# State space output of a hybrid layer: products packed by channel pair, one activation per batch instead of sixteen

## The chip, the core and the metric

One core of a Trainium2 chip runs the whole program. The metric is the device time of one execution in microseconds, the median of three runs. The engines are named as the profile names them: PE is TensorE (matrix products; PEld are its weight loads), DVE is VectorE, ACT is ScalarE, POOL is GpSimd, SP is SyncE, which here only issues transfers.

## The reference, cut to what matters

One decoder layer with two parallel groups, a state space group (SSM) and a latent attention group (MLA), then a gated MLP. The change touches the last step of the SSM group:

```
s_re, s_im = associative_scan(...)            # 64 channel groups of 16, state of 64 each
y = (einsum('lbgp,ghp->blgh', s_re, c_re)
     - einsum('lbgp,ghp->blgh', s_im, c_im)
     + d_skip * u)
y = gelu(y)                                   # 256 tokens x 1024 channels
y_ssm = y * sigmoid(y @ w_glu + b_glu)
```

## The kernel before, in words

The layer has 256 tokens and 2048 channels, in float32 throughout. A large product is made of three: each 128x1024 chunk of weights is split by ACT (`hi`, line 150) and DVE (`lo`, line 151), and PE multiplies in the order of lines 165, 166 and 168. Before about 284 us the program is the input projection, the attention with the SSM beside it, and the output projections; after it come the up and down products of the MLP (lines 175, 177 and 1132), where PE hardly waits.

The SSM's 64 groups are 32 pairs, worked through in 8 batches b of 4 pairs q. A pair has 32 channels. The scan runs over 64 blocks i of 4 tokens j. Of each batch the functions do this:

- `ssm_v` (line 533): PE, 16 products into a bank `psv`, out of `gm`, which DVE transposes in `ssm_in_mats` (line 490).
- `ssm_k` (line 544): PE, 8 products of 32 columns; `ssm_m` (lines 557, 561) makes out of them the matrix `mt`, by DVE and 8 copies of ACT.
- `ssm_rot` (lines 571 to 587): rotation and scan on DVE, ending in `sh` (line 587); `ssm_back` (lines 595 to 599): POOL turns it back into the states `spv`.
- `ssm_y` (lines 610 to 619): the output. It adds three products, `mt` by the inputs `u4`, and the matrix `clp` by both halves of `spv`, into a bank `psy`, and ACT writes gelu of it into `yT`.

`ssm_main` strings these together in three steps per batch; `pace()` takes steps between the chunks of the other work, by a table of digits (`STEPS`). The order in which each engine finally gets its instructions is set by the framework's scheduler when the program is built, by its own estimate of when each could run; on the chip each engine runs its list strictly in that order. So a change of one function moves instructions of others.

Around the SSM stand: the last steps of the attention heads (lines 921 to 955; `macc` collects the sums of squares on POOL); `tok_sums`, `tok_rsqrt`, `tok_rows` (lines 260, 267, 268, 275), which turn `macc` into the scale row `rr` (copied by ACT at line 998); `out_mla` (lines 165 to 168 on tiles `ym`, then DVE at lines 1000 and 1001), whose results wait in three `mm` banks for `rr`; and, when all of `yT` is there, its split into `yhl` (lines 1018, 1019) and eight products with `w_glu` (lines 165 to 168 on tiles `yhl`), whose squares POOL adds into `sacc`, summed by PE at line 260.

Of the kernel before, what the change touches and what calls it, by code (L numbers as in the profile page):

```python
# [14 lines left out]
AF = mybir.ActivationFunctionType  # L15
# [8 lines left out]
T = 256  # L24
# [30 lines left out]
def layer_kernel(ctx: ExitStack, tc: tile.TileContext, pack, pos, xt, bk, w_in, w_kpe, w_uqn,  # L55
                 w_uqp, w_kn, w_v, w_glu, w_out, w_up, w_down, final_w, out):
    nc = tc.nc
    V, A, G_, PE, SP = nc.vector, nc.scalar, nc.gpsimd, nc.tensor, nc.sync
# [10 lines left out]
    def wk_bank():  # L69
        return psw.tile([P, 512], F32, tag="wk", name="wk")  # L70
# [440 lines left out]
    u4_ = [None]  # L511
# [12 lines left out]
    psvs, psks, yT = {}, {}, [None]  # L524
# [76 lines left out]
    def ssm_y(b):  # L601
        if b == 0:
            yT[0] = mid.tile([P, 8, T], F32, tag="mB", name="yT")
        qs = slice(4 * b, 4 * b + 4)
        m, s, clp = mt[b % 2], spv[b % 2], clps[b % 4]
        psy = wk_bank().rearrange("p (q i) -> p q i", i=64)
        for q in range(4):
            for hf in range(2):
                hp = slice(64 * hf, 64 * hf + 64)
                PE.matmul(psy[hp, q], m[:, q, 2 * hf:2 * hf + 2].rearrange("p j n -> p (j n)"),  # L610
                          u4_[0][:, b, q, :], start=True, stop=False)
                for c in range(2):
                    PE.matmul(psy[hp, q],
                              clp[:, c, q, 2 * hf:2 * hf + 2].rearrange("p l g h -> p (l g h)"),
                              s[:, c, q, :], start=False, stop=(c == 1))
        for q in range(4):
            dst = yT[0][32 * q:32 * q + 32, b].rearrange("p (i j) -> p j i", j=4)
            for j in range(4):
                A.activation(dst[:, j], psy[32 * j:32 * j + 32, q], AF.Gelu_apprx_tanh)  # L619

    def ssm_main():

        for b in range(9):
            ssm_load(b + 1)
            if b < 8:
                ssm_v(b)
            if b < 7:
                ssm_out_mats(b + 1, 0)
            yield
            if b < 8:  # L630
                ssm_rot(b)
                ssm_k(b)
            if b < 7:
                ssm_in_products(b + 1)
                ssm_out_mats(b + 1, 1)
            yield
            if b > 0:
                ssm_y(b - 1)
            if b < 8:
                ssm_back(b)  # L640
                ssm_m(b)
            if b < 7:
                ssm_in_mats(b + 1)
            yield
# [109 lines left out]
    for i, (ct, hf) in enumerate(u_order):  # L754
# [12 lines left out]
        if i >= 7:  # L767
            while done:
                c = done.pop(0)
# [132 lines left out]
    def scratch(kind):  # L902
        o, n = ring[kind]
        turn[kind] ^= 1
        o += n * turn[kind]
        return scr[:, o:o + n]
# [137 lines left out]
    for ct in range(16):  # L1044
# [3 lines left out]
        t = scratch("t")  # L1048
# [17 lines left out]
    for i in range(44):  # L1066
        pgv = [mm_bank(), wk_bank()]
        a = abuf[i % 2]
        for gv, hf in up_order(i):
# [3 lines left out]
            if hf == 1:  # L1073
                t = fp.tile([P, T], F32, tag=f"cv{gv}", name="low")
# [7 lines left out]
        for gv in range(2):  # L1082
            ch_ = 44 * gv + i
            t = fp.tile([P, T], F32, tag=f"cv{gv}", name="cv")
# [198 lines left out]
```

## Time and profile before

| | |
|---|---|
| time, median of 3 runs | 1097.57 us (1096.87 to 1098.04) |
| the profiled execution: its time, its span | 1098.27 us, 1096.4 us |
| busy over the span: PE, PEld | 1053.3 us (96%), 930.4 us (85%) |
| DVE, ACT, POOL | 771.4 us (70%), 626.7 us (57%), 269.6 us (25%) |

How to read it: the shares are means over the span. PE is close to always busy, but its 4% of idle time is not spread evenly, and neither is the work of the others; what the change can move lies in the first quarter of the span, so the rows below are cut by stage. A row of a timeline gives the start, how long the merged instructions took from the first start to the last end, the engine, the line, what it writes and reads, how many were merged (x16), and in brackets how long the engine had sat idle before it, and for whom. A float32 product shows as two records of PE, each with a weight load of its own. PEclk is the share of TensorE's full clock of 2.4 GHz that was granted; the lower level is 1.2 GHz, so 0.92 is a mixture.

### The profile page before, as it was taken

Reading aid. Unit: us, or ns where it says so; the run is one execution under the profiler, and the core shown is the slowest. Engines: PE = TensorE matmul, PEld = TensorE weight load, DVE = VectorE, ACT = ScalarE, POOL = GpSimd, SP = SyncE. Lnnn points to the kernel's source line nnn. Section 1 sums busy time; section 2 is a strip of 40 time slices with the busy share of each in tenths; the row PEclk is TensorE's granted clock in tenths of the full one; section 3 lists DMA queues with packets and bytes.
Section 4 is the critical chain, followed back from the end, with each engine's and each line's share of the span. In section 5 each row is a group of like instructions: output and inputs, shape, how many; then the busy total and the mean of one; then the engine's idle time right before and its main releaser. Section 6 shows DMA issues by size and latency. Waiting matters only on the chain.

```text
span 1096.4 us, 18029 instructions
## 1 busy us (share of the span) xinstructions
PE 1053.3 (96%) x6856; PEld 930.4 (85%) x6856; DVE 771.4 (70%) x1085; ACT 626.7 (57%) x1074; POOL 269.6 (25%) x284
## 2 busy tenths in 40 slices
PE   7979999878999999999999999999999999999997
PEld 7978878777999888888888888888888888888896
DVE  8999898697799677676767676676768445454543
ACT  6567688947766565555655555555555434343433
POOL 8371645674234111111121212111111000000000
PEclk9989999999999999999999999999999999999999
DMA  6645432542655566666666666666666976666662
GB/s 211 220 116 182 141 115 78 173 134 79 198 179 185 171 195 192 189 192 184 191 183 195 190 190 186 184 193 188 193 182 187 247 247 187 188 184 191 213 190 77
DMA packets 56663, 195.24 MB, mean 178 GB/s; under 512 B 6528, under 2 KB 8448, under 8 KB 56576
## 3 DMA queue, kind: packets, MB, share of 16 engines
q1 hardware_dynamic: 54576, 190.93, 56.8%
q10 hardware_dynamic: 2000, 3.16, 1.3%
q8 instruction: 54, 0.88, 0.3%
q14 instruction: 33, 0.27, 0.1%
HBM read 189.86 MB, written 2.10 MB: 175 GB/s over the span
## 4 chain that ended last, share of the span: by engine, by line
PE 78%; DVE 10%; ACT 6%; issue 3%; DMA 3%; POOL 0%; ACTq 0%; SPq 0%; DVEq 0%
PE mm L175 15%; PE wk L175 15%; PE mm L1132 11%; PE wk L1132 11%; PE wk L177 8%; PE mm L177 8%; PE mm L168 3%; PE mm L166 3%; PE mm L165 3%; DVE lo L151 2%; ACT yT L619 2%; DMA raw<-in_w_in_dram 1%; ACT hi L150 1%; DVE epad L486 1%; PE wk L922 1%
## 5 line engine op out<-in xcount | busy, mean ns | idle before, releaser
L151 DVE TENSOR_TENSOR lo<-raw,hi 128x1024 fp32r<-128x1024 f32 x329 | 411.0, 1251 | 267.5 <-ACT hi L150 259.9
L150 ACT CAST hi<-raw 128x1024 fp32r<-128x1024 f32 x329 | 343.8, 1048 | 320.4 <-PE wk L1132 113.3
L1093 POOL TENSOR_TENSOR cv<-cv 128x256 f32<-128x256 f32 x44 | 51.6, 1173 | 395.5 <-ACT cv L1092 395.5
L175 PE MATMUL mm<-x2b,hi 128*128 128x512 f32 x352 | 88.3, 392 | 0.0
L175 PE MATMUL wk<-x2b,hi 128*128 128x512 f32 x352 | 88.3, 392 | 0.0
L175 PE MATMUL mm<-x,hi 128*128 128x512 f32 x352 | 88.2, 392 | 0.0
L175 PE MATMUL wk<-x,hi 128*128 128x512 f32 x352 | 88.1, 392 | 0.0
L1132 PE MATMUL wk<-hi,hid 128*128 128x512 f32 (+1 forms) x360 | 88.0, 364 | 0.0
L1132 PE MATMUL mm<-hi,hid 128*128 128x512 f32 x312 | 85.5, 396 | 0.0
L1132 PEld LDWEIGHTS wk<-hi,hid 128*128 128x128 f32 x360 | 63.5, 188 | 13.0
L175 PEld LDWEIGHTS wk<-x2b,hi 128*128 128x128 f32 x352 | 63.4, 189 | 11.3
L175 PEld LDWEIGHTS mm<-x,hi 128*128 128x128 f32 x352 | 63.3, 189 | 11.3
L175 PEld LDWEIGHTS mm<-x2b,hi 128*128 128x128 f32 x352 | 63.3, 189 | 11.3
L175 PEld LDWEIGHTS wk<-x,hi 128*128 128x128 f32 x352 | 63.3, 189 | 11.3
L1132 PEld LDWEIGHTS mm<-hi,hid 128*128 128x128 f32 x312 | 57.8, 188 | 13.2 <-ACT hi L150 0.2
L177 PEld LDWEIGHTS mm<-x2b,lo 128*128 128x128 f32 x352 | 48.1, 190 | 3.4
L177 PEld LDWEIGHTS wk<-x,lo 128*128 128x128 f32 x352 | 48.0, 190 | 3.4
L177 PEld LDWEIGHTS mm<-x,lo 128*128 128x128 f32 x352 | 48.0, 190 | 3.4
L177 PEld LDWEIGHTS wk<-x2b,lo 128*128 128x128 f32 x352 | 48.0, 190 | 3.4
L1132 PE MATMUL wk<-lo,hid 128*128 128x512 f32 (+1 forms) x180 | 50.9, 364 | 0.0
L165 PE MATMUL mm<-xh,hi 128*128 128x256 f32 x184 | 47.9, 294 | 2.5 <-ACT hi L150 2.5
L1094 ACT CAST hid<-cv 128x256 fp32r<-128x256 f32 x44 | 17.9, 406 | 55.6 <-POOL cv L1093 55.6
(345 smaller groups left out, 2152.6 us busy)
## 6 DMA issues: line engine op xcount, KB each, us to landing
raw<-in_w_up_dram SPq DMA_DIRECT2D x176, 512.0 KB, 3.7
raw<-in_w_down_dram SPq DMA_DIRECT2D x88, 512.0 KB, 3.7
raw<-in_w_out_dram SPq DMA_DIRECT2D x32, 512.0 KB, 3.7
raw<-in_w_in_dram SPq DMA_DIRECT2D x25, 512.0 KB, 4.0
bkt<-in_bk_dram SPq DMA_DIRECT2D x8, 512.0 KB, 5.6
raw<-in_w_glu_dram SPq DMA_DIRECT2D x8, 512.0 KB, 4.2
raw<-in_w_uqn_dram SPq DMA_DIRECT2D x4, 512.0 KB, 4.0
hT<-in_xt_dram SPq DMA_DIRECT2D x4, 512.0 KB, 5.3
```

What stands on the lines that cost most here:

```text
L150: A.copy(hi, raw)
L151: V.tensor_tensor(out=lo, in0=raw, in1=hi.bitcast(F32), op=ALU.subtract)
L165: PE.matmul(ps, wh(k), xh(k), start=(first and k == 0), stop=False)
L166: PE.matmul(ps, wh(k), xl(k), start=False, stop=False)
L168: PE.matmul(ps, wl(k), xh(k), start=False, stop=(last and k == nk - 1))
L175: PE.matmul(ps, wh(k), xp(k), start=(first and k == 0), stop=False)
L177: PE.matmul(ps[:, n:], wl(k), xp(k)[:, 0], start=False, stop=(last and k == nk - 1))
L486: V.tensor_tensor(out=epad[:, :, g, :, g, :], in0=ev1[:, :, g], in1=ev2[:, :, g], op=ALU.add)
L619: A.activation(dst[:, j], psy[32 * j:32 * j + 32, q], AF.Gelu_apprx_tanh)
L1093: G_.tensor_tensor(out=cv[0], in0=cv[0], in1=cv[1], op=ALU.mult)
L1094: A.copy(hid[0][:, i, :], cv[0])
L1132: PE.matmul(ps[:, 0:n], hid[x][:, 2 * i + k, ts_], w[wk][:, 512 * k + c0:512 * k + c0 + n], start=(i == 0 and s == 0 and k == 0), stop=(i ...
```

## The change

Before, the two tokens of a half (hf) were taken together: a product gave 64 partitions (2 tokens of 32 channels) of `psy`, at a place in the bank for each pair q. Each piece of 32 partitions by 64 columns then had to go to other partitions of `yT`, so ACT needed 16 activations of 32x64. Now each product gives one token j of one pair q, 32 partitions by 64 columns, at partitions 32q, where `yT` has that pair; 48 products take the place of 24, and one activation of 128x256 that of 16. Summed values and their order stay.

```diff
-        psy = wk_bank().rearrange("p (q i) -> p q i", i=64)
-        for q in range(4):
-            for hf in range(2):
-                hp = slice(64 * hf, 64 * hf + 64)
-                PE.matmul(psy[hp, q], m[:, q, 2 * hf:2 * hf + 2].rearrange("p j n -> p (j n)"),
-                          u4_[0][:, b, q, :], start=True, stop=False)
-                for c in range(2):
-                    PE.matmul(psy[hp, q],
-                              clp[:, c, q, 2 * hf:2 * hf + 2].rearrange("p l g h -> p (l g h)"),
-                              s[:, c, q, :], start=False, stop=(c == 1))
-        for q in range(4):
-            dst = yT[0][32 * q:32 * q + 32, b].rearrange("p (i j) -> p j i", j=4)
-            for j in range(4):
-                A.activation(dst[:, j], psy[32 * j:32 * j + 32, q], AF.Gelu_apprx_tanh)
+        psy = wk_bank()[:, 0:T].rearrange("p (j i) -> p j i", j=4)
+
+        for j in range(4):
+            for t in range(3):
+                for q in range(4):
+                    w = m[:, q, j] if t == 0 else clp[:, t - 1, q, j].rearrange("p g h -> p (g h)")
+                    PE.matmul(psy[32 * q:32 * q + 32, j], w, u4_[0][:, b, q, :] if t == 0 else s[:, t - 1, q, :],
+                              start=(t == 0), stop=(t == 2))
+        A.activation(yT[0][:, b].rearrange("p (i j) -> p j i", j=4), psy, AF.Gelu_apprx_tanh)
```

The file is five lines shorter below this place: a line L1000 of before is L995 after, and the output's lines 610, 613 and 619 become 612, 612 and 614. The scheduler, given other lengths for these instructions, orders the engines' lists anew between about 130 and 310 us. Two places matter.

The first is DVE's list from the reciprocal of `tok_rsqrt` (line 268) on, where `out_mla`'s first results are taken out of their banks (lines 1000 and 1001; 995 and 996 after). Before:

```order
L268 RECIPROCAL rtok<-rtok 128x2
L151 TENSOR_TENSOR lo<-raw,hi 128x1024 x3
L1000 TENSOR_TENSOR scr<-mm,rr 128x256 x2
L578 TENSOR_TENSOR ta<-wk,tabc 128x512
L579 TENSOR_TENSOR tb<-wk,tabc 128x512
L480 TENSOR_TENSOR e_2474<-bkt,wkk 128x512
L557 TENSOR_TENSOR wk<-wk,bkt 32x2x32
L1001 TENSOR_TENSOR hT<-hT,scr 128x256 x2
```

and now:

```order
L268 RECIPROCAL rtok<-rtok 128x2
L151 TENSOR_TENSOR lo<-raw,hi 128x1024 x2
L995 TENSOR_TENSOR scr<-mm,rr 128x256 x2
L996 TENSOR_TENSOR hT<-hT,scr 128x256 x2
L578 TENSOR_TENSOR ta<-wk,tabc 128x512
L579 TENSOR_TENSOR tb<-wk,tabc 128x512
L480 TENSOR_TENSOR e_2501<-bkt,wkk 128x512
L557 TENSOR_TENSOR wk<-wk,bkt 32x2x32
```

One of three `lo` has moved behind the first results. From line 268 to the last scan (line 587 of batch 7) DVE's list held 11 each of `lo`, `scr` and `hT`, and now holds 10 of each; the eleventh stand behind the scan.

The second is the end of ACT's list in this stage: the copies to the last `mt` (line 561, batch 7), the gelu of batches 6 and 7, and the split of `yT` (line 1018; 1013 after). Before:

```order
L561 COPY mt_125<-wk 32x2x128 x2
L561 COPY mt_125<-wk 32x2x96
L619 ACTIVATE yT<-wk 32x64 x16
L561 COPY mt_125<-wk 32x2x96
L561 COPY mt_125<-wk 32x2x64 x2
L561 COPY mt_125<-wk 32x2x32 x2
L150 CAST hi<-raw 128x1024
L1018 CAST yhl<-yT 128x512 x3
L150 CAST hi<-raw 128x1024 x2
L619 ACTIVATE yT<-wk 32x64 x16
L1018 CAST yhl<-yT 128x512
```

and now:

```order
L561 COPY mt_125<-wk 32x2x128 x2
L561 COPY mt_125<-wk 32x2x96 x2
L561 COPY mt_125<-wk 32x2x64 x2
L561 COPY mt_125<-wk 32x2x32 x2
L614 ACTIVATE yT<-wk 128x4x64
L150 CAST hi<-raw 128x1024
L1013 CAST yhl<-yT 128x512 x3
L150 CAST hi<-raw 128x1024
L614 ACTIVATE yT<-wk 128x4x64
L1013 CAST yhl<-yT 128x512
```

The copies now stand together ahead of batch 6's gelu, and one `hi` fewer stands ahead of batch 7's. In PE's list, counted the same way, 240 of the 128x256 products of lines 165 to 168 stand between `rr`'s products (line 275) and the end of batch 7's output products, where there were 260. From there on to the sum of `sacc` (line 260), which was the 259th product on, there are now 275, and the sum itself stands 7 products further ahead in the work: 282 to the same place.

## Rows read from the trace of the kernel before

**Rows 1.** By stage: length, busy PE, PEld, DVE, ACT, POOL, clock, DMA share, GB/s

```profile
130.00:184.00 54.00, 51.30 (x387) 42.09 (x387) 49.62 (x100) 40.94 (x100) 30.82 (x34) 1.00 0.38 118
...
184.00:205.40 21.40, 17.74 (x224) 16.33 (x222) 9.22 (x22) 20.24 (x61) 10.50 (x14) 0.92 0.34 124
205.40:262.00 56.60, 47.04 (x613) 43.93 (x613) 56.09 (x77) 34.66 (x93) 41.46 (x40) 0.94 0.40 122
...
262.00:284.00 22.00, 18.77 (x161) 17.27 (x160) 11.61 (x17) 18.87 (x49) 4.00 (x4) 0.92 0.36 125
```

**Rows 2.** Timeline of ACT around the scale row rr

```profile
198.26 4.64 ACT L619 ACTIVATE yT<-wk 32x64 f32<-32x64 f32 x16
202.92 1.28 ACT L267 ACT_TABLE_LOAD   x1
...
207.21 0.37 ACT L998 COPY rr<-wk 128x256 f32<-128x256 f32 x1
```

**Rows 3.** Timeline of DVE: behind rtok, and the last scan

```profile
204.51 0.17 DVE L268 RECIPROCAL rtok<-rtok 128x2 f32<-128x2 f32 x1 [7.14 <-ACT rtok L267]
205.44 4.83 DVE L151 TENSOR_TENSOR lo<-raw,hi 128x1024 fp32r<-128x1024 f32 x3 [0.77 <-ACT hi L150]
210.19 0.74 DVE L1000 TENSOR_TENSOR scr<-mm,rr 128x256 f32<-128x256 f32 x2
...
260.56 1.22 DVE L587 TENSOR_TENSOR_SCAN sh<-d,vh 128x512 f32<-128x512 f32 x1
```

**Rows 4.** Groups by line and shape: count, busy us, mean ns, idle before

```profile
L151 DVE TENSOR_TENSOR lo<-raw,hi 128x1024 fp32r<-128x1024 f32 x102 | 133.2, 1310 | 41.3 <-ACT hi L150 34.7 <-PE mm L168 2.9 <-ACT r L282 1.9
...
L619 ACT ACTIVATE yT<-wk 32x64 f32<-32x64 f32 x128 | 35.6, 278 | 8.3 <-PE wk L613 6.8
...
L1001 DVE TENSOR_TENSOR hT<-hT,scr 128x256 f32<-128x256 f32 x16 | 10.7, 678 | 0.0
...
L1000 DVE TENSOR_TENSOR scr<-mm,rr 128x256 f32<-128x256 f32 x16 | 6.4, 414 | 0.1
...
L953 ACT ACTIVATE scr<-wk 128x256 f32<-128x256 f32 x8 | 3.2, 395 | 3.5 <-PE wk L951 3.4
```

**Rows 5.** Timeline of ACT, POOL and PE in the last two batches

```profile
261.70 4.61 ACT L619 ACTIVATE yT<-wk 32x64 f32<-32x64 f32 x16
...
265.35 0.73 POOL L599 TENSOR_TENSOR spv<-td,tc__3122 128x252 f32<-128x252 f32 x1
...
277.47 0.62 PE L165 MATMUL mm<-yhl,hi 128*128 128x256 f32 x3 [1.77 <-ACT yhl L1018]
...
305.63 0.50 PE L260 MATMUL wk<-ones,sacc 128*128 128x1 f32 x4
```

**Rows 6.** Timeline of PE: small products, and full ones, without a wait

```profile
189.58 0.60 PE L950 MATMUL wk<-scr,qv 128*128 128x256 f32 x2
190.02 0.38 PE L951 MATMUL wk<-scr,qv 128*128 128x128 f32 x2
...
204.82 0.68 PE L275 MATMUL wk<-ident,rtok 128*128 128x128 f32 x4 [0.65 <-DVE rtok L268]
205.44 1.15 PE L533 MATMUL wk<-u,gm 128*64 128x64 f32 x32
206.52 1.07 PE L544 MATMUL wk<-clp,bkt 128*32 128x128 f32 x16
207.51 0.33 PE L610 MATMUL wk<-u,mt 128*64 128x64 f32 x2
...
208.85 0.45 PE L613 MATMUL wk<-spv,clp 128*64 128x64 f32 x6
...
288.47 1.12 PE L168 MATMUL mm<-yhl,lo 128*128 128x256 f32 x8
```

**Rows 7.** Timeline of PE behind batch 0's output; waits of PE, 184 to 282 us

```profile
139.59 0.38 PE L165 MATMUL mm<-chl,hi 128*128 128x256 f32 x1 [1.66 <-ACT qpt L889]
...
PE wk L533 <- DVE gm L490: 7.4, 3, 3.1
```

## The prediction

> **What bounds the kernel now.** I read the stages first [rows 1], then the timelines of the engine that each stage names. The change touches only about 130 to 284 us; behind it PE works without a pause, so whatever PE starts earlier there ends earlier at the end.
>
> - 130 to 184 us: PE is busy 51.30 of 54.00 us, ACT only 40.94. PE is the bound.
> - 184 to 205.4 us: ACT is busy 20.24 of 21.40 us and is the bound; two of the eight gelu blocks lie here. One of them stands right in the way [rows 2]: the activations of batch 2 from 198.26 to 202.92, and only then the root `rtok`. DVE waits 7.14 us for it [rows 3].
> - 205.4 to 262 us: DVE is busy 56.09 of 56.60 us. It is the bound; ACT has 22 us to spare. PE waits, 7.4 us in three waits for `gm`, which comes from DVE [rows 7].
> - 262 to 284 us: DVE drops to 11.61 of 22.00, ACT is busy 18.87. Batch 6's 16 activations [rows 5], from 261.70 to 266.31, cut the copies to the last `mt` in two, batch 7's follow, and PE waits 1.77 us for the last split at 277.47.
>
> **Part by part.**
>
> *Gelu.* 128 activations at 278 ns, 35.6 us in all; back to back, 16 take 4.64 us [rows 2, 4]. The nearest single activation of 128x256 out of a bank is line 953 at 395 ns [rows 4]. The strided write into `yT` may cost more: all of the 278 ns by its 64 columns, taken four times, would be 1.1 us. I take 0.45, since the 395 reads as many values from the same memory; ACT is freed of about 4.2 us a batch. In the first stage this hides behind PE, in the third behind DVE; it counts in the second and fourth.
>
> *The products.* Each batch had 48 records on PE and now has 96, each still streaming 64 columns. Before, they took from 207.51 to 209.30, 1.79 us [rows 6]. What do records of 32 partitions cost? No row has them with four column groups taking turns. The neighbours [rows 6]: line 533, 64 columns, two groups in turn: (1.15 - 0.22)/31 = 30 ns per record, the 0.22 being one record's own length. Line 544, 128 columns, two groups of 32: (1.07 - 0.27)/15 = 53 ns. A full-width product, 256 columns: line 951 starts 0.44 us after line 950's two records, 220 ns each, so 55 ns for 64 columns if nothing runs beside it. Hence the ends: no overlap, 96 x 55 ns and some 0.35 us to start and drain = 5.6 us; four side by side, 96 x 14 ns and 0.35 = 1.7 us. I take 30 ns, the rate of line 533, as the closest in columns streamed and in width: 96 x 0.030 + 0.35 = 3.2 us, **1.4 us more per batch** (ends -0.1 and 3.9).
>
> Lines 533 and 544 show 64 columns at 30 ns and 128 at 53, so the columns streamed set the pace there. The Trainium skill ("TensorEngine Tiling (Array Packing)", Performance Considerations) says that a product has about 60 cycles of overhead, so that one of a single column takes as long as one of 60, and that the tiling factor should not be taken from a dimension that is already small; this speaks against the change. By its 60 cycles at 2.4 GHz, 25 ns by estimate, a batch would take 2.75 us and cost 1.0 more. No run here shows the floor yet.
>
> *130 to 184 us.* Batch 0's products become 1.4 us longer, ahead of a wait of 1.66 us of PE for ACT [rows 7], which hides them; without that cover they would cost all 1.4. Gain and loss: 0.
>
> *184 to 205.4 us.* ACT gives up 8.4 of 20.24 us. The next bound is PE: 17.74 busy and 2 x 1.4 make 20.5 of 21.40 [rows 1], so the products of line 275 come only about 1 us earlier, ending at 204.4 in place of 205.5 [rows 6], and `rr`, 0.37 us [rows 2], at 204.8. But what stood between is gone: before, three `lo` (4.83 us) came between the root and the first `scr`, at 210.19 [rows 3], because their `hi` wait on ACT behind the root. With `rtok` no longer behind 16 activations, the two `lo` that still stand ahead run while PE works, and `scr` starts at 204.8.
>
> *205.4 to 262 us.* From that `scr` to the last scan's end, 261.78, DVE had 51.6 us without a pause [rows 3]. The third `lo` now lies in it, +1.3; and one `lo`, `scr` and `hT` each of the list have gone behind the scan, -(1.3 + 0.4 + 0.7) = -2.4 by their means [rows 4]. So the scan ends at 204.8 + 51.6 + 1.3 - 2.4 = 255.3, if DVE need never wait for PE. PE has 47.04 [rows 1] + 4 x 1.4 - 20 moved products at 0.12 us (eight records of line 168 start within 0.84 us of each other [rows 6]) = 50.2 us of work in 50.9: next to no slack, although a clock of 0.94 in that stage [rows 1] may give back up to 3 us of it if PE idles less. I charge 2 us of DVE waiting for PE: 257.3, a gain of 4.5.
>
> *262 us on.* After the scan POOL needs 4.3 us for the last `spv` (266.08 against 261.78 [rows 3, 5]), then the products 3.2 us: 264.8. Gelu and the last split follow while PE works off what remains of the chunks, so its waits here go. To the place of the sum of `sacc` PE has 282 products at 0.12 us, 33.8 us: 298.6 instead of 305.63 [rows 5].
>
> The sum: **7 us less**. Made against the profiled execution, 1098.27 us (its span is 1096.4), which is 0.7 above the median of 1097.57, that is 1091.3; against the median, **1090.5**.
>
> **The rivals.**
>
> 1. *Four groups truly side by side.* Then the products cost what they did. For it: line 544, 32 wide, paces itself by half the full-width rate with two groups, so four may halve it again. Against: 30 ns is the smallest spacing in these rows. PE no longer bounds 184 to 205.4 (1.4 x 2 = 2.8 us come back), the 2 us charged for DVE's waits go, and batch 7's own 1.4: 7 + 6 = 13 us, 1084.5. The Trainium skill (same page, Performance Considerations, on column tiling) gives up to 4x for products of 32 columns. That is this rival.
>
> 2. *The products don't overlap, the other side.* At 55 ns per record a batch costs 3.9 us more; PE's work in the second and third stage becomes 17.74 + 7.8 and 47.04 + 15.6 - 2.4, 85.8 us in 78: 8 us more, and batch 0's pokes 2.2 out of its cover; against that stands up to 5 us of waits in the tail. About 5 us slower, 1102.5. It decides from where the added time eats PE's waits: 3.66, 9.56 and 3.2 us idle in the last three stages [rows 1] over seven batches, 2.3 us each, a record at 39 ns. For it: twice as many loads of weights. Against: line 544, whose groups of 32 do overlap.
>
> 3. *The waits come back elsewhere.* PE goes through its list strictly in order; the moved `ssm_v` may stand at the head of it and wait for `gm` as before, with DVE then waiting for PE's chunks. Only the tail's gain would be left, and part of it eaten by longer products: 0 to 3 us less, 1096. For it: 7.4 us of such waits now [rows 7], and PE without slack. Against: DVE's list is shorter, and it starts on it earlier.
>
> That the change doesn't do what it says is no case here: the list shows one gelu per batch.
>
> **How the numbers follow.** Chances: forecast 0.56, rival 1 0.19, rival 2 0.09, rival 3 0.13, and 0.03 for a slower outcome of another kind. The time is that of the forecast, 1090.5; its own ends, by charges of 0 to 4 us in the third stage and 1.0 for the products, are 1087 to 1094. The range reaches into rivals 1 and 3: 1083 to 1096.5. A measurement of this kernel tells about 0.2%, 2.2 us, from no change. Faster by more: forecast, rival 1 and half of rival 3, 0.82; the same: most of the rest of rival 3 and a little of rival 2, 0.08; slower, 0.10.
>
> **What would show it.** The span between the first and the last record of a batch's products: 3.2 us, not 1.7 or 5.6. One gelu of 128x256 at 0.4 to 0.6 us. `rtok` some 5 us earlier, and `rr` at about 205. DVE without its 7 us wait, the last scan near 257 us. PE busier than 0.95 of 205 to 257 us. No wait of 1.77 us for `yhl`. If `rr` comes early and the scan does not, rival 3 has it; if a batch takes over 4 us, rival 2.

## The result and the profile after

| | before, beside it | after |
|---|---|---|
| time, median | 1097.80 us (1096.87 to 1098.32, 4 runs) | 1091.74 us (1090.89 to 1093.39, 4 runs) |
| ratio | | 0.9943 (95% interval 0.9932 to 0.9955) |
| span of the profiled execution | 1096.4 us | 1090.7 us |

6.1 us faster, where 7 were forecast; 1091.74 lies in the range. The profiled execution of the changed kernel is its slowest (1093.39 us), so I compare spans and places in them.

The stages of the changed kernel (columns as in [rows 1]; the cuts now lie where `rr` is due, where the last scan ends, and at the sum of `sacc`):

```profile
130.00:184.00 54.00, 50.07 (x433) 40.51 (x429) 49.04 (x93) 36.50 (x85) 30.14 (x33) 1.00 0.38 121
184.00:202.40 18.40, 16.86 (x327) 15.52 (x327) 12.35 (x30) 14.32 (x34) 12.31 (x15) 1.00 0.37 122
202.40:256.80 54.40, 46.20 (x798) 42.89 (x797) 52.62 (x74) 22.23 (x46) 41.06 (x40) 0.91 0.40 126
256.80:298.80 42.00, 39.95 (x398) 39.07 (x397) 34.45 (x45) 27.32 (x49) 16.86 (x14) 0.96 0.56 182
```

In the second stage ACT no longer leads (14.32 of 18.40 us; it had 20.24 of 21.40). In the third DVE does (52.62 of 54.40), and PE has 8 us free. Now the single places. ACT around `rr` and in the last batches, answering to [rows 2, 5]:

```profile
198.44 0.63 ACT L614 ACTIVATE yT<-wk 128x256 f32<-128x256 f32 x1
200.38 0.26 ACT L267 ACTIVATE rtok<-wk,eps_t 128x2 f32<-128x2 f32 x1
203.37 0.37 ACT L993 COPY rr<-wk 128x256 f32<-128x256 f32 x1
...
258.04 0.65 ACT L614 ACTIVATE yT<-wk 128x256 f32<-128x256 f32 x1
260.38 1.66 ACT L1013 CAST yhl<-yT 128x512 fp32r<-128x512 f32 x3 [0.83 <-POOL td L596]
265.32 0.64 ACT L614 ACTIVATE yT<-wk 128x256 f32<-128x256 f32 x1 [2.33 <-PE wk L612]
```

DVE, answering to [rows 3]:

```profile
200.68 0.17 DVE L268 RECIPROCAL rtok<-rtok 128x2 f32<-128x2 f32 x1 [2.34 <-ACT rtok L267]
201.61 3.39 DVE L151 TENSOR_TENSOR lo<-raw,hi 128x1024 fp32r<-128x1024 f32 x2 [0.77 <-ACT hi L150]
204.92 0.74 DVE L995 TENSOR_TENSOR scr<-mm,rr 128x256 f32<-128x256 f32 x2
...
255.53 1.22 DVE L587 TENSOR_TENSOR_SCAN sh<-d,vh 128x512 f32<-128x512 f32 x1
```

PE: two of the products with the head values, the products of batch 2 from the first to the last row, and the sum of `sacc`, answering to [rows 5, 6]:

```profile
185.44 0.60 PE L945 MATMUL wk<-scr,qv 128*128 128x256 f32 x2
191.82 0.60 PE L945 MATMUL wk<-scr,qv 128*128 128x256 f32 x2
194.65 0.32 PE L612 MATMUL wk<-u,mt 128*32 128x64 f32 x8
...
195.79 0.41 PE L612 MATMUL wk<-spv,clp 128*32 128x64 f32 x16
...
298.82 0.50 PE L260 MATMUL wk<-ones,sacc 128*128 128x1 f32 x4
```

And PE's waits from 184 us to the sum of `sacc`, answering to [rows 7]:

```profile
PE wk L533 <- DVE gm L490: 3.4, 3, 1.6
PE wk L612 <- POOL spv L598: 3.1, 2, 2.1
PE mm L165 <- DVE scr L995: 2.6, 2, 2.0
PE wk L260 <- POOL macc L910: 1.5, 1, 1.5
PE wk L612 <- POOL spv L599: 1.0, 1, 1.0
```

| place | before | forecast | after |
|---|---|---|---|
| a batch's products, first to last | 1.79 us | 3.2 us | 1.55 us |
| a batch's gelu | 4.64 us | 0.45 us | 0.64 us |
| first `scr` | 210.19 | 204.8 | 204.92 |
| last scan's end | 261.78 | 257.3 | 256.75 |
| batch 7's products done | 269.0 | 264.8 | 265.3 |
| sum of `sacc` | 305.63 | 298.6 | 298.82 |

So the places where time was to be won came out within 0.6 us. But two terms on the way were off: the products cost 1.55 us and not 3.2, and the two head values now stand 2.0 and 2.2 us later than before (183.46 and 189.58 before, the second in [rows 6]), where nothing was forecast. In a second trace of the same kernel (e7) they stand at 184.66 and 191.04, 1.2 and 1.5 us later than before, so part of that lateness is the spread between executions. The sum came out since errors of both signs cancelled. The experiments ask what each of them is worth.

### The profile page after: what moved, and what is told of

Same layout as the page of the kernel before. It is cut to its first block, busy times and chain, and to the rows that moved or that the text cites. A ratio compares the mean times of both kernels' runs of the same rounds, so it can differ in the third digit from the quotient of the medians.

```text
span 1090.7 us, 18676 instructions
## 1 busy us (share of the span) xinstructions
PE 1053.7 (97%) x7240; PEld 931.4 (85%) x7240; DVE 774.8 (71%) x1085; ACT 596.7 (55%) x954; POOL 274.2 (25%) x284
## 4 chain that ended last, share of the span: by engine, by line
PE 80%; DVE 9%; issue 3%; POOL 3%; DMA 2%; ACT 2%; SPq 0%; ACTq 0%; DVEq 0%; POOLq 0%
PE mm L175 15%; PE wk L175 15%; PE mm L1127 11%; PE wk L1127 11%; PE wk L177 8%; PE mm L177 8%; PE mm L168 3%; PE mm L166 3%; PE mm L165 3%; DVE lo L151 3%; DMA bkt<-in_bk_dram 1%; DMA raw<-in_w_in_dram 1%; ACT u L521 1%; DVE epad L486 1%; POOL td L596 1%
## 5 line engine op out<-in xcount | busy, mean ns | idle before, releaser
L177 PE MATMUL mm<-x2b,lo 128*128 128x256 f32 x352 | 49.3, 282 | 0.0
```

Of the source, the lines that this page charges most:

```text
L177: PE.matmul(ps[:, n:], wl(k), xp(k)[:, 0], start=False, stop=(last and k == nk - 1))
```

## Experiments

Times are medians, ratios against the kernel before run on the same chip. A useful cut for all of them is the last scan's end and the way from there to the sum of `sacc`:

| run | time, us | ratio (interval) | last scan's end | from there to `sacc` | PEclk, 262 to 284 us |
|---|---|---|---|---|---|
| before | 1097.8 to 1098.2 | | 261.78 | 43.9 | 0.92 |
| after | 1091.74 | 0.9943 (0.9932 to 0.9955) | 256.75 | 42.1 | 0.92 |
| e7 after again | 1092.12 | 0.9946 (0.9935 to 0.9958) | 256.29 | 42.0 | 0.92 |
| e1 activation alone | 1089.73 | 0.9925 (0.9912 to 0.9937) | 259.52 | 38.1 | 1.00 |
| e2 products alone | 1088.95 | 0.9922 (0.9910 to 0.9935) | 258.07 | 39.0 | 1.00 |
| e4 another order of products | 1093.25 | 0.9962 (0.9949 to 0.9975) | 259.02 | 39.8 | 1.00 |
| e5 batch 0 as before | 1089.86 | 0.9927 (0.9913 to 0.9941) | 255.07 | 40.5 | 1.00 |
| e6 e2 with slow activations | 1099.78 | 1.0016 (1.0006 to 1.0026) | 261.25 | 44.6 | 0.92 |
| e8 additions on POOL | 1093.41 | 0.9960 (0.9947 to 0.9972) | 255.87 | 44.4 | 0.88 |
| e10 e2, no gaps | 1088.74 | 0.9917 (0.9903 to 0.9930) | 257.00 | 38.3 | 1.00 |
| e11 fast in batches 1, 2 | 1095.20 | 0.9975 (0.9966 to 0.9984) | 257.99 | 44.4 | 0.92 |
| e12 fast in 3, 4, 5 | 1098.97 | 1.0012 (1.0002 to 1.0022) | 262.38 | 44.6 | 0.92 |
| e13 fast in 6, 7 | 1094.31 | 0.9966 (0.9953 to 0.9978) | 262.16 | 39.0 | 1.00 |

The last column is the clock granted to PE in the profiled execution of each, as in [rows 1]. It matters in what follows: where it was 1.00, the way from the scan to `sacc` took 40.5 us or less, and where it was lower, 42.0 or more. By estimate, 22 us at 0.92 hold 1.8 us less of PE's work than 22 us at 1.00 (22 x 0.08). That is nearly the whole of several differences of 2 to 3 us below.

### Each half of the change by itself

e1 keeps the products of before and puts one activation behind them:

```diff
-        for q in range(4):
-            dst = yT[0][32 * q:32 * q + 32, b].rearrange("p (i j) -> p j i", j=4)
-            for j in range(4):
-                A.activation(dst[:, j], psy[32 * j:32 * j + 32, q], AF.Gelu_apprx_tanh)
+        A.activation(yT[0][:, b].rearrange("p (i j) -> p j i", j=4), psy, AF.Gelu_apprx_tanh)
```

> The activation alone: the products of before (24 of 64 columns of weights), and one activation of 128x256 per batch over them. The move of the pieces to their partitions is left out, so yT gets the right number of values at wrong places; all else runs as it is. Theory A (ACT's time is the whole gain, the new products cost nothing): as the changed kernel, 1091.7, within 1.5 us. Theory B (the new products cost 1.4 us per batch, as the prediction priced them, and eat a part of the gain): some 4 to 6 us faster than the changed kernel, 1086 to 1088. Theory C (the new products themselves give part of the gain): 1094 or more.

e2 has the new products, and puts 16 activations behind them in place of one:

```diff
-        A.activation(yT[0][:, b].rearrange("p (i j) -> p j i", j=4), psy, AF.Gelu_apprx_tanh)
+        yq = yT[0][:, b].rearrange("p (i j) -> p j i", j=4)
+        for q in range(4):
+            for j in range(4):
+                A.activation(yq[32 * q:32 * q + 32, j], psy[32 * q:32 * q + 32, j], AF.Gelu_apprx_tanh)
```

> The products alone: 48 products in four column groups per batch, and 16 activations of 32x64 behind them as before. Theory A: as the kernel before, 1097.8, within 1.5 us, the batch of records taking 1.55 to 1.6 us. Theory B: 4 to 8 us slower than before, 1102 to 1106. Theory C: 1095 or less.

e1 took 1089.73 us and e2 1088.95: either half alone gives the whole gain and 2 to 3 us more, with intervals that just overlap those of the changed kernel. Neither gets this ahead of the scan, which ends 1.3 to 3.2 us later than in the two traces of the changed kernel; both get it behind the scan, where the clock was 1.00. Theory A missed e1 by 2.0 us, 0.5 more than its margin, and failed on e2, which was to be as slow as before. Theories B and C missed at least one of the two as well. The reason for e2 stands in its rows of ACT:

```profile
188.86 2.56 ACT L617 ACTIVATE yT<-wk 32x64 f32<-32x64 f32 x16
197.04 2.53 ACT L617 ACTIVATE yT<-wk 32x64 f32<-32x64 f32 x16
200.88 0.26 ACT L267 ACTIVATE rtok<-wk,eps_t 128x2 f32<-128x2 f32 x1
```

As many activations of the same shape as before, and they take 2.56 us and not 4.64 [rows 2]. So e2 frees ACT as well, of 2.1 us a batch. Whether that makes the gain, or the lists that the scheduler ordered anew, e2 can't tell.

### The same lists, with fast or slow activations

e6 is e2, but each activation reads the quarter of partitions that it read before the change:

```diff
-                A.activation(yq[32 * q:32 * q + 32, j], psy[32 * q:32 * q + 32, j], AF.Gelu_apprx_tanh)
+                A.activation(yq[32 * q:32 * q + 32, j], psy[32 * j:32 * j + 32, q], AF.Gelu_apprx_tanh)
```

> The kernel of the run e2 (the new products, 16 activations of 32x64), but each activation reads another quarter of the partitions than it writes, as before the change; the lists of all engines are those of e2, row by row. So a part is left out: the values stand at wrong places of yT. In e2 one of the 16 took 160 ns, in the kernel before 278 to 290 ns, 2.1 us per batch. Theory F (crossing to other partitions costs those 2.1 us, and ACT's time is what set e2's gain of 9 us): 4.6 us per batch again, the root of rtok about 2 x 2.1 = 4 us later than in e2, the sum of sacc 4 to 6 us later, and 1093 to 1097. Theory G (the re-ordered lists made e2's gain, not ACT's time): 1089 to 1090, whatever the activations take.

```profile
188.00 4.64 ACT L617 ACTIVATE yT<-wk 32x64 f32<-32x64 f32 x16
197.85 4.63 ACT L617 ACTIVATE yT<-wk 32x64 f32<-32x64 f32 x16
203.79 0.26 ACT L267 ACTIVATE rtok<-wk,eps_t 128x2 f32<-128x2 f32 x1
```

1099.78 us, 10.8 more than e2, with the same instructions in the same order on every engine. Theory F holds, and by more than it said: ACT's 2.1 us a batch are worth 10.8 us, and the new products and lists by themselves give nothing (1.0016 of before, 1.0006 to 1.0026).

Which batches? Three kernels with these lists make the activations fast in some batches only (the tuple is `(1, 2)`, `(3, 4, 5)` or `(6, 7)`):

```diff
-                A.activation(yq[32 * q:32 * q + 32, j], psy[32 * q:32 * q + 32, j], AF.Gelu_apprx_tanh)
+                pi, ci = (q, j) if b in (1, 2) else (j, q)
+                A.activation(yq[32 * q:32 * q + 32, j], psy[32 * pi:32 * pi + 32, ci], AF.Gelu_apprx_tanh)
```

> Lists as in e2 and e6, row by row. The activations of batches 1 and 2 read and write the same quarter (2.55 us per batch, as e2), those of the other batches read another quarter (4.63 us, as e6); those others land at wrong places of yT. The prediction's first place: the activations ahead of the root of rtok, two batches, 4.1 us of ACT. If that place carries its share as the prediction had it: rtok and the first scr about 4 us earlier than in e6, the last scan 3 to 4 us earlier, and 4 to 5 of the 10.8 us between e6 and e2: 1095.

> As the run of batches 1 and 2, but batches 3, 4 and 5 are the fast ones. Their activations lie where DVE was busy 56.43 of 57.00 us in e6 and ACT has 22 us to spare. The prediction: hidden there, so as e6, 1099 to 1100. The rival: ACT's list is strict, so copies and hi behind the activations come earlier and PE or DVE with them, 1 to 3 us less.

> As the run of batches 1 and 2, but batches 6 and 7 are the fast ones: the prediction's second place, the last batches, where ACT was busy 18.11 of 22.00 us in e6. If that place carries what is left: 4 to 6 us less than e6, 1094 to 1096. If the tail is hidden while the scan is late: less than 2 us, 1098.

Against e6: 4.6 us from batches 1 and 2, 0.8 from 3 to 5 (the intervals of e12 and e6 lie almost on each other), 5.5 from 6 and 7. Together 10.9, against 10.8 us between e6 and e2: the places add up, and nothing is left for batch 0. The ratios, which take out the difference between chips, say the same: 0.0095 in sum, 0.0094 between e6 and e2. e11's last scan, and its sum of `sacc`:

```profile
256.77 1.22 DVE L587 TENSOR_TENSOR_SCAN sh<-d,vh 128x512 f32<-128x512 f32 x1
...
302.34 0.50 PE L260 MATMUL wk<-ones,sacc 128*128 128x1 f32 x4
```

and e13's:

```profile
260.94 1.22 DVE L587 TENSOR_TENSOR_SCAN sh<-d,vh 128x512 f32<-128x512 f32 x1
...
301.19 0.50 PE L260 MATMUL wk<-ones,sacc 128*128 128x1 f32 x4
```

e11 ends its scan as early as e2 and then needs as long as e6 (44.4 us); e13 ends it as late as e6 and then needs as long as e2 (39.0). That is the prediction's pair of places, the one ahead of `rtok` and the one in the last batches, each by itself. In the second, e6's waits of PE behind the scan name the path, and all of them but 0.7 us are gone in e13:

```profile
PE mm L165 <- ACT hi L150: 2.8, 1, 2.8
PE mm L166 <- DVE yhl L1017: 1.1, 2, 1.0
```

Batch 6's and 7's activations stand in ACT's list ahead of `hi` and `yhl`, for which PE then waits. These waits, 3.9 us in e6 and 0.7 in e13, are 3.2 of the 5.6 us by which e13's way from the scan to `sacc` is shorter. The rest is PE's own busy time on that way, 40.56 us in e6 and 38.24 in e13, at another clock (first e6, then e13, columns as in [rows 1]):

```profile
262.00:284.00 22.00, 17.95 (x201) 16.56 (x201) 10.80 (x15) 18.11 (x47) 3.46 (x4) 0.92 0.37 124
262.00:284.00 22.00, 21.21 (x251) 20.44 (x246) 15.91 (x22) 18.57 (x57) 6.07 (x6) 1.00 0.54 183
```

e10 shortens the activations of e2 further, by a write without gaps:

```diff
-        yq = yT[0][:, b].rearrange("p (i j) -> p j i", j=4)
+        yq = yT[0][:, b].rearrange("p (j i) -> p j i", j=4)
```

> The kernel of e2, lists the same row by row, but the 16 activations write yT without gaps, so values stand at wrong places of yT. In e9 the write without gaps took 0.39 us in place of 0.64 for 256 columns, so about 1 us of ACT less per batch than in e2 by estimate, 1.5 to 1.6 us in place of 2.55. If ACT's time still sets the pace as between e6 and e2 (10.8 us for 2.1 us per batch): 5 us less than e2, 1084. If the gain is used up once ACT has those 2.1 us per batch: as e2, 1088 to 1089.

They took 2.20 us, only 0.35 less than e2's, not 1; the time is 1088.74. By the rate between e6 and e2, 0.35 us a batch would be 1.8 us less (10.8/2.1 x 0.35); 0.2 was measured, which leans to a used-up gain but is too small a step to show it. For the same side speaks the changed kernel: 1.9 us a batch less of ACT than e2, and not faster; but its lists are others, and so is its clock behind the scan, so this is an argument and not a test. There the root comes at 200.38 in place of e2's 200.88, only 0.5 us earlier, and PE's sum ahead of it waits 1.5 us for POOL's `macc` in both.

### What an activation's place costs

e9 has another form of the gelu in each batch, 16 or 4 or one, as its expectation lists them.

> The changed kernel with another form of the gelu in each batch, so that one trace shows what each form takes; in batches 1, 4 and 7 the values land at wrong places of yT. Batch 1: 16 of 32x64 that cross partitions and write every fourth value. 2: 16 that don't cross, pair by pair. 3: 16 that don't cross, the quarter of the partitions changing each time. 4: one of 128x256 that writes without gaps. 5: four of 32x256. 6: four of 128x64. 7: 16 that cross and write without gaps. If crossing is what costs: batches 1 and 7 at 280 ns each, 2 and 3 at 160. If it is the change of quarter from one to the next: 3 as 1. If the gaps in the write cost: batch 4 at 0.4 us in place of 0.64, and 7 cheaper than 1.

ACT in batches 1 to 7 of e9, in one execution:

```profile
190.01 4.63 ACT L619 ACTIVATE yT<-wk 32x64 f32<-32x64 f32 x16
199.89 2.55 ACT L623 ACTIVATE yT<-wk 32x64 f32<-32x64 f32 x16
208.55 4.65 ACT L627 ACTIVATE yT<-wk 32x64 f32<-32x64 f32 x16
230.18 0.39 ACT L629 ACTIVATE yT<-wk 128x256 f32<-128x256 f32 x1 [1.41 <-PE wk L612]
242.99 2.57 ACT L632 ACTIVATE yT<-wk 32x256 f32<-32x256 f32 x4 [2.91 <-PE wk L612]
262.25 0.65 ACT L635 ACTIVATE yT<-wk 128x64 f32<-128x64 f32 x4
268.17 3.63 ACT L639 ACTIVATE yT<-wk 32x64 f32<-32x64 f32 x16 [1.75 <-PE wk L612]
```

Batch 3 (4.65 us) crosses no partitions and is as slow as batch 1, so it isn't the crossing; a crossing that stays on one quarter was not run. It reads another quarter with each activation, as batch 1 does; batch 2 stays in one quarter for four. The line's own durations in e9 say where the time goes, first batch 2's, then batch 3's:

```profile
L623 ACT ACTIVATE yT<-wk x16: 267/280/301, 199.9 to 202.1; 32x64 f32<-32x64 f32 x16
```

```profile
L627 ACT ACTIVATE yT<-wk x16: 275/280/284, 208.5 to 212.9; 32x64 f32<-32x64 f32 x16
```

One activation takes 280 ns in both; the 160 ns of two expectations are 2.55 us divided by 16, and not the length of one. In batch 3 each starts (4.65 - 0.28)/15 = 291 ns behind the one before it, when that is done. In batch 2 the mean of the 15 steps is 151 ns, but they are of two kinds: twelve stay within a quarter, where the next one starts 104 to 126 ns behind while the last still runs, and three change the quarter and take 296 to 308 ns (single starts of the trace). Four of 128x64 over all partitions overlap as well (0.65 us, batch 6), four of 32x256 in four quarters do not (2.57 = 4 x 0.64, batch 5). And the gaps cost by themselves: a write of 256 columns takes 0.39 us without them and 0.64 with a value every 16 bytes. This also says why e10 gained only 0.35 us. Its activations take 198 to 218 ns and not 280, but within a quarter they start 103 to 125 ns apart, as in e2; only the three changes of quarter and the last activation became shorter. Where every activation waits for the last, the write without gaps saved 1.0 us (batch 7, 3.63 us, against batch 1).

### The products' price

e4 is the changed kernel with two loops exchanged, so that three products of one quarter follow each other:

```diff
-            for t in range(3):
-                for q in range(4):
+            for q in range(4):
+                for t in range(3):
```

> The changed kernel with its 48 products in another order: the three products of one pair, which share their 32 partitions of the bank, directly behind each other, and only then the next pair. The lists of the other engines stay as they are, to a few rows. If the records overlap only because neighbours in the list write different column groups: 96 records at 30 to 55 ns, a batch of 3 to 5.6 us in place of 1.55, and 4 to 10 us slower than the changed kernel, 1096 to 1102. If any order of 32-wide products overlaps as well: 14 ns per record and 1091.7.

Batch 2 of e4, first and last row:

```profile
194.48 0.30 PE L612 MATMUL wk<-u,mt 128*32 128x64 f32 x2
...
196.71 0.42 PE L612 MATMUL wk<-spv,clp 128*32 128x64 f32 x6
```

From 194.48 to 197.13 are 2.65 us. A record has a length of 0.22 us of its own, so the starts are on average (2.65 - 0.22)/95 = 26 ns apart; in the changed kernel (1.55 - 0.22)/95 = 14 ns; in the kernel before (1.79 - 0.22)/47 = 33 ns. The single starts come in sets: in the changed kernel four records within 20 ns, and the next four 56 ns behind the first four; in the kernel before two records, and the next two 58 ns behind. So the order is what makes 48 products as cheap as 24 were, and both ends of the expectation, 3 to 5.6 us a batch and 14 ns a record, missed. Three products of one quarter also add into the same values, and e4 can't tell the one from the other. The kernel became 1.1 to 1.5 us slower (1093.25 against 1092.12 and 1091.74; the intervals of the ratios overlap) for 1.1 us a batch, 8.8 us of PE in all. Its scan ends 2.3 to 2.7 us later, and the clock of 1.00 behind it gave some of that back; a few rows of ACT's and DVE's lists moved too.

### The lists before 190 us, and DVE's load behind

e5 is the changed kernel with batch 0 as before the change, which leaves the lists up to batch 1's output as they were:

```diff
+        if b == 0:
...
+            return
         psy = wk_bank()[:, 0:T].rearrange("p (j i) -> p j i", j=4)
```

> The changed kernel, but batch 0 with the products and the 16 activations of before. Up to batch 1's output the lists of all engines then stand as before the change (DVE's up to the 267th row). Theory D (the attention stretch ended about 2 us later after the change because the lists were ordered anew there, and that lateness went through to the end): the products of the head values at 183.5 and 189.6 us again, and about 2 us faster than the changed kernel, 1089.7. Theory E (that lateness was taken up behind it, since DVE sets the pace from 205 us on): no difference, 1091.7 within 1.

1089.86 us, against 1091.74, and against 1092.12 in a second measurement of the changed kernel:

> The changed kernel once more, beside the others of this call, to see how far the 1089 to 1090 of e1, e2 and e5 stand from it: 1091.7 within 1 us if they differ; 1090 or less if all four are the same.

Theory D: the head values in e5 come at 183.81 and 189.97 us, and the sum of `sacc` at 295.60 in place of 298.82 and 298.27:

```profile
183.81 0.60 PE L962 MATMUL wk<-scr,qv 128*128 128x256 f32 x2
189.97 0.60 PE L962 MATMUL wk<-scr,qv 128*128 128x256 f32 x2
...
295.60 0.50 PE L260 MATMUL wk<-ones,sacc 128*128 128x1 f32 x4
```

The intervals of the ratios just overlap (0.9913 to 0.9941 and 0.9932 to 0.9955), so 2 us is the size, not its second digit. And theory D holds for a part of it only. Against e7 the head values are 0.9 and 1.1 us earlier and the last scan ends 1.2 us earlier (1.7 against the first trace). Another 1.5 us come behind the scan, where PE waits the same 2.0 us for `spv` in both and the clock differs (first e5, then e7):

```profile
262.00:284.00 22.00, 22.00 (x221) 21.91 (x211) 17.19 (x25) 13.90 (x24) 5.10 (x5) 1.00 0.68 225
262.00:284.00 22.00, 21.54 (x237) 21.37 (x238) 16.23 (x23) 12.52 (x22) 4.29 (x5) 0.92 0.65 210
```

What gave e5 that clock these runs don't show.

e8 takes five additions from DVE:

```diff
-        V.tensor_tensor(out=hT[:, ct, :], in0=hT[:, ct, :], in1=t, op=ALU.add)
+        (G_ if ct < 10 and ct % 2 else V).tensor_tensor(out=hT[:, ct, :], in0=hT[:, ct, :], in1=t, op=ALU.add)
```

> The changed kernel, with five of the ten additions into hT that stand between rr and the last scan moved from DVE to POOL (odd chunks below 10): DVE has 5 x 0.67 = 3.3 us less to do there, POOL some 5 x 1 us more of its 12 us of free time. Theory H (DVE is still the bound from 205 to 257 us): last scan 2 to 3 us earlier and 1089 to 1090. Theory I (PE's chunks, in order behind waits for gm and spv, or POOL, have become the bound): scan no more than 1 us earlier and 1091 to 1093.

The scan ended at 255.87 us, 0.4 before that of e7, with 3.3 us less work on DVE, and 1093.41 us came out, 0.4 above the range of theory I, which is the nearer one. POOL is now the fullest after DVE, and the clock is lower than in the changed kernel:

```profile
205.00:262.00 57.00, 46.42 (x791) 43.00 (x783) 52.26 (x71) 23.62 (x51) 50.36 (x48) 0.89 0.37 111
262.00:284.00 22.00, 22.00 (x211) 21.83 (x204) 14.95 (x22) 11.20 (x18) 3.71 (x3) 0.88 0.64 211
```

In e7 the same two stages had 0.94 and 0.92. PE's waits behind the scan are the same (2.1 us, 2.0 in e7), and its busy time from the scan to `sacc` is 42.28 us against 39.94, so the tail of 44.4 us in place of 42.0 is PE working slower. That POOL's load brought the clock down is not tested, and a few rows of e8's lists stand elsewhere too.

## Why the prediction was right, and where not

*What bounds the kernel.* Right, and shown on the lists of e2: the gain of freeing ACT lies ahead of `rtok` (e11, 4.6 us) and in the last batches (e13, 5.5 us); in between it is hidden (e12, 0.8, within the noise). Of the 5.5 us some 2.3 are PE's faster records, which the prediction did not have there. The term "the scan ends at 257.3, a gain of 4.5" met 256.75, and 1.3 of the 2 us charged for DVE's waits were there: one wait for POOL's `spv`, in the row "DVE tb L579" of DVE's waits.

*Gelu, 0.45 us.* It took 0.64: the gaps of the write, which I had named and set aside, cost 0.25 us. That changed nothing, as ACT had room.

*The products, 1.4 us more per batch.* The step that failed. The rate of line 533, 30 ns, was taken "as the closest in columns streamed and in width"; what decides is how many quarters take turns, and with four of them a record takes 14 ns. A batch became 0.2 us shorter. The prediction weighed a rule against the change: the Trainium skill ("TensorEngine Tiling (Array Packing)", Performance Considerations) has an overhead of some 60 cycles for each product. At 2.4 GHz that is 25 ns per record by estimate; 14 ns lies below it, so the measurement decides. The 4x that the same section of the Trainium skill has for column tiling with products of 32 columns is nearer: from the 55 ns that the prediction worked out at full width to 14 ns is a factor of 3.9.

*Rival 1* had that rate, and 1084.5. Its price failed: it gave back 6 us for 1.4 us a batch, but in e4 1.1 us a batch made 1.1 to 1.5 us in all, 2.3 to 2.7 by the scan's end. Both it and my "next to no slack" took PE for nearly full from 205 to 257 us; it was busy 46.20 of 54.40, 0.85 and not over 0.95.

*130 to 184 us: 0.* Wrong by 1 to 2 us: in e5 the scan ends 1.2 to 1.7 us earlier. I looked at what the longer products would cost behind batch 0 and not at how the lists around the attention heads were ordered anew.

*The tail.* "After the scan POOL needs 4.3 us" became 6.1. The 80 records of batch 7 behind it took 2.34 us, where the same 80 took 1.32 in e5. PE had worked 0.88 of the 2.90 us ahead of them, and the clock granted then was 0.54 of 2.4 GHz, so nearly all at the lower level of 1.2 GHz (windows of the changed kernel, columns as in [rows 1]):

```profile
262.80:265.30 2.50, 2.37 (x81) 2.21 (x81) 2.16 (x4) 0.18 (x1) 0.07 (x1) 0.54 0.57 205
260.00:262.90 2.90, 0.88 (x12) 0.39 (x10) 2.90 (x4) 2.52 (x4) 2.79 (x3) 1.00 0.52 181
```

The idle time alone does not settle it: in e5 PE had worked 0.90 of the 2.90 us from 258.30 on, and 1.00 was granted behind it. Why the clock fell here stays open. Here again the errors cancel: 264.8 forecast, 265.3 measured. The wait of 1.77 us for `yhl` is gone, as forecast.

*Rival 3* took its part: PE's waits for `gm` fell from 7.4 to 3.4 us (5.3 in e7), and 4.1 us of waits for `spv` came in.

*The change itself.* As far as the time of the kernel shows, what it paid for before was neither the number of activations nor their size, as I had it, but that each read another quarter than the one before it. The new places of the products end that, even with 16 activations. e2, with them, is the fastest of the versions that leave nothing out: 1088.95 us, 2.8 below the changed kernel. Its lists ahead of 190 us are not the reason: the head values (183.88 and 190.41) are 0.8 and 0.6 us earlier than in e7, but the last scan ends 1.8 us later. It gains 3.0 us behind the scan, where PE waits 0.7 in place of 2.0 us and the clock is 1.00 in place of 0.92. Whether its lists bring that clock with them wasn't tested.

## What to carry to other kernels

Cost a chain of small activations by what stands next to what: keep neighbours on the same partitions, and they overlap. Ask for each place where an engine is freed who is next there, since 10.1 of 10.8 us came from four of eight batches here, and the freed time beyond 2 us a batch bought nothing that these runs could show. And where a scheduler orders the lists, an edit moves work far from itself: to separate the two, change a duration and not the lists (as e6 does to e2). Before a difference of 2 us is given a cause, compare the clock of the stages: here it alone makes nearly as much.

## What the hardware showed that I had not expected

- ACT: activations of 32x64 that read the same quarter of the partitions start 104 to 126 ns apart, those that change it 291 ns, each 280 ns long (e9). Without gaps in the write each takes 198 to 218 ns, and within a quarter the starts stay as far apart (e10). A write with 16 bytes between values took 0.64 us in place of 0.39 for 256 columns. The Trainium skill ("SBUF — State Buffer", Door 1: The DMA port swizzle) says that consecutive accesses to the same 16-byte line go at full rate and that each access that crosses to a new line costs. These rows agree.
- PE: records of 64 columns start on average 14 ns apart when four column groups of 32 take turns, 26 ns when three products in a row share a group (e4), 33 ns with groups of 64 and three in a row (before).
- The lower clock behind that wait of PE: 24 of batch 7's records took 0.64 us, 24 of batch 2's 0.33 (clock 0.54 and 1.00).
